# Output projection and ConvFFN as 2x2 blocks in seven products, with the gated activations in HBM between the FFN halves

## The chip, the core and the metric

The kernel runs on one core of one Trainium2 chip. The metric is the device time of one execution in microseconds (us). The engines are named as in the profile: PE (TensorE, matrix products; its weight loads are listed as PEld), DVE (VectorE), ACT (ScalarE), POOL (GpSimd) and SP (SyncE, whose queue issues every DMA of this kernel). PSUM is where PE writes its products, SBUF is the working memory of the core, HBM the memory outside.

## What is computed

One layer of a streaming encoder, for a prompt of 1024 tokens and 64 tokens of a running stream ("samples"), model width 1024. After two mixers (retention and gated linear attention, four heads each) come the parts that the change touches:

```
mix = concatenate([o_r, o_g])                         # 1024 wide
x   = x + g1 * (mix @ w_out)                          # w_out 1024 x 1024
h2  = rmsnorm(x) * (1 + sc2) + sh2
a, up = split(h2 @ w_ffn_in)                          # w_ffn_in 1024 x 5632, D_FF = 2816
conv = conv_b + sum_j conv_w[j] * a[t - 2 + j]        # causal, width 3
y   = silu(conv) * up
x   = x + g2 * (y @ w_ffn_out)                        # w_ffn_out 2816 x 1024
out = rmsnorm(x)
```

All inputs and outputs are fp32.

## The kernel before, in words

Activations are held with the features on the 128 partitions and the tokens as columns, in three chunks c of 384, 384 and 320 columns (the last one: 256 prompt tokens and the 64 samples). A product in nearly full precision takes three matmuls: operand and weight are each split into a high part (a rounded copy, by ACT) and a low part (the rest, a subtraction, by DVE or POOL), and `mm3` (line 247) issues high x high, high x low and low x high into one PSUM bank for each block of 128 features. All matmuls go through `mm` (line 238, the profile's L239), all transposes through `tr` (L244), and ACT, DVE and POOL instructions through one wrapper (L91), so the profile tells them apart by their tiles.

Weights come as units of 512 KB in their order of use (`plan`, lines 598 to 618): `load_unit` issues the DMA, `split_unit` the ACT copy, and its low part follows on DVE. A `flow` object counts estimated PE time as instructions are emitted and gives side streams (generators) a step whenever their delay has passed, so that norms, evictions and loads are emitted between products.

Around the change, in order of emission: the gate of retention head 3 is projected chunk by chunk, and `split_mix` (line 1365) splits the mixed features of each chunk that is ready. The output projection (lines 1454 to 1498) loops over chunks and, within a chunk, over the eight output blocks m; every block has its weight unit loaded again for each chunk (24 units). Its result is scaled by the gate G1 and added to x, which PE has transposed; squares are summed for the norm. When a chunk is complete, `norm2` (line 1418) starts as a side stream: the sum over partitions by PE, a reciprocal root in 12 small DVE instructions (`rsqrt_steps`), its broadcast by PE, and the split of the normed chunk. The next chunk's products run meanwhile.

The ConvFFN (lines 1644 to 1668) loops over 22 blocks f of 128 features, in pairs: `ev_a` and `conv` make the convolution branch, `ev_u` multiplies with the up projection and splits the result, and `ffn_out` (line 1554) multiplies the two blocks of the pair before with their rows of w_ffn_out and adds the scaled result into x2, which stays in SBUF. Only one pair of blocks of y exists at a time. In the last pair the squares and the final norm (`final`, line 1598) follow chunk by chunk.

## Time and profile before

| | |
|---|---|
| median of 3 runs | 1528.62 us (1527.5 to 1533.15) |
| span of the profiled execution, first to last instruction | 1527.1 us |
| PE busy | 1440.4 us, 94%, 9062 matmuls |
| DVE, ACT, POOL busy | 902.2, 486.7, 349.6 us |
| read from HBM, written | 98.23 MB, 5.29 MB |

The profile holds one execution; its own time is its span (the profile has no other time of it), and the median of the runs lies 1.5 us above that. Busy times of the engines overlap. A matmul's duration in the profile covers its passage through the array, and the next one starts before it ends, so the distance between starts tells how fast PE works. "Idle before, releaser" names what ended a wait.

### The profile page before, as it was taken

What the parts mean: (1) busy time and instruction counts of PE and PEld (TensorE: products, weight loads), DVE (VectorE), ACT (ScalarE), POOL (GpSimd) and SP (SyncE); (2) the same over time, 40 slices, a digit from 0 to 9 for tenths busy, and PEclk for the clock granted to TensorE, in tenths of its full rate; (3) what the DMA queues carried; (4) which work ended last, traced back from release to release, by engine and by line L of the source; (5) the groups of instructions that cost most, each with busy time, mean ns of one, the idle gap of its engine ahead of it and who ended that gap; (6) DMA issues with size and microseconds to landing.
All of it is one profiled execution on the core that took longest, in us unless ns stands there. A gap on an engine that the chain in (4) does not pass through costs nothing.

```text
span 1527.1 us, 22788 instructions
## 1 busy us (share of the span) xinstructions
PE 1440.4 (94%) x9062; PEld 1393.9 (91%) x9062; DVE 902.2 (59%) x1754; ACT 486.7 (32%) x979; POOL 349.6 (23%) x423
## 2 busy tenths in 40 slices
PE   5999888989989899899999999999999999999997
PEld 3778778879879899899999999999999999999996
DVE  6637878957885888567644445362535454444445
ACT  5635344433233325454412121212121212112136
POOL 3335424414332443222110000000010101010024
PEclk9999999999999999999999999999999999999999
DMA  8420102123223222454111110101111111111103
GB/s 257 156 62 15 56 9 67 42 82 99 87 87 99 79 81 67 148 149 135 54 42 42 42 56 29 55 29 56 56 39 46 42 42 56 41 43 42 42 2 118
DMA packets 128336, 104.98 MB, mean 69 GB/s; under 512 B 5129, under 2 KB 114535, under 8 KB 128231
## 3 DMA queue, kind: packets, MB, share of 16 engines
q1 hardware_dynamic: 128231, 103.53, 22.2%
q8 instruction: 71, 1.16, 0.3%
q14 instruction: 34, 0.28, 0.1%
HBM read 98.23 MB, written 5.29 MB: 68 GB/s over the span
## 4 chain that ended last, share of the span: by engine, by line
PE 70%; DVE 15%; issue 5%; ACT 3%; POOL 1%; DMA 0%; DVEq 0%; POOLq 0%; ACTq 0%
PE mm L239 38%; PE o L239 16%; PE sc L239 15%; DVE qbd L91 2%; DVE att L91 1%; DVE acc L91 1%; PE sc L244 1%; DVE t L91 1%; DVE ra L91 1%; DVE b L91 1%; DVE on L91 1%; ACT on L91 1%; DVE lo L91 1%; DVE sbd L91 1%; POOL acc L91 1%
## 5 line engine op out<-in xcount | busy, mean ns | idle before, releaser
L239 PE MATMUL mm<-act_hi,hi 128*128 128x384 f32 (+1 forms) x1152 | 393.0, 341 | 0.3 <-DVE mix L91 0.2
L239 PE MATMUL mm<-act_hi,lo 128*128 128x384 f32 (+1 forms) x1152 | 379.4, 329 | 4.2 <-DVE lo L91 4.2
L239 PE MATMUL mm<-act_lo,hi 128*128 128x384 f32 (+1 forms) x1152 | 378.7, 329 | 0.1
L239 PEld LDWEIGHTS mm<-act_hi,lo 128*128 128x128 f32 x1152 | 218.3, 190 | 4.7 <-DVE lo L91 4.5
L239 PEld LDWEIGHTS mm<-act_hi,hi 128*128 128x128 f32 x1152 | 219.3, 190 | 1.9 <-DVE mix L91 0.5
L239 PEld LDWEIGHTS mm<-act_lo,hi 128*128 128x128 f32 x1152 | 219.0, 190 | 0.8 <-POOL act_lo L91 0.3
L91 DVE TENSOR_TENSOR lo<-raw,hi 128x1024 fp32r<-128x1024 f32 x115 | 144.4, 1264 | 93.5 <-ACT hi L91 93.4
L91 ACT CAST hi<-raw 128x1024 fp32r<-128x1024 f32 x118 | 121.7, 1042 | 224.1 <-issue 192.4
L91 DVE TENSOR_SCALAR cv<-ab,cw 128x1090 f32<-128x1090 f32 x22 | 18.7, 849 | 188.0 <-ACT ab L91 186.3
L91 DVE SCALAR_TENSOR_TENSOR x<-mm,G,x 128x384 f32<-128x384 f32 (+2 forms) x201 | 95.7, 498 | 51.2 <-PE mm L239 39.5
L91 POOL TENSOR_TENSOR yl<-yf,yh 128x384 fp32r<-128x384 f32 (+1 forms) x66 | 63.1, 969 | 225.9 <-ACT yh L91 225.9
L91 POOL COPY tails<-ab 128x2 f32<-128x2 f32 x44 | 6.8, 189 | 459.4 <-ACT ab L91 459.4
L239 PE MATMUL sc<-act_hi,lo 128*128 128x384 f32 (+1 forms) x288 | 94.1, 327 | 0.0
L239 PE MATMUL sc<-act_lo,hi 128*128 128x384 f32 (+1 forms) x288 | 94.1, 327 | 0.0
L239 PE MATMUL sc<-act_hi,hi 128*128 128x384 f32 (+1 forms) x288 | 94.1, 327 | 0.0
L239 PE MATMUL o<-act_hi,lo 128*128 128x384 f32 (+1 forms) x288 | 93.7, 325 | 0.0
L239 PE MATMUL o<-act_hi,hi 128*128 128x384 f32 (+1 forms) x288 | 93.7, 325 | 0.0
L239 PE MATMUL o<-act_lo,hi 128*128 128x384 f32 (+1 forms) x288 | 93.6, 325 | 0.0
L239 PE MATMUL mm<-hi,act_hi 128*128 128x256 f32 x288 | 87.8, 305 | 0.2 <-ACT hi L91 0.2
L239 PE MATMUL mm<-lo,act_hi 128*128 128x256 f32 x288 | 82.6, 287 | 3.0 <-DVE lo L91 3.0
L239 PE MATMUL mm<-yh,hi 128*128 128x384 f32 (+1 forms) x254 | 84.1, 331 | 1.0 <-DVE na L91 0.6
L239 PE MATMUL mm<-yh,lo 128*128 128x384 f32 (+1 forms) x254 | 83.5, 329 | 0.0
(247 smaller groups left out, 3038.2 us busy)
## 6 DMA issues: line engine op xcount, KB each, us to landing
raw<-in_w_ffn_in_dram SPq DMA_DIRECT2D x44, 512.0 KB, 3.8
raw<-in_w_ada_dram SPq DMA_DIRECT2D x32, 512.0 KB, 4.0
raw<-in_w_in_dram SPq DMA_DIRECT2D x28, 512.0 KB, 3.8
raw<-in_w_out_dram SPq DMA_DIRECT2D x24, 512.0 KB, 3.9
raw<-in_w_ffn_out_dram SPq DMA_DIRECT2D x22, 512.0 KB, 4.7
wa<-in_w_ada_dram SPq DMA_DIRECT2D x16, 512.0 KB, 4.8
xs<-in_x_prompt_dram SPq DMA_DIRECT2D x8, 512.0 KB, 7.2
out_dram<-yt SPq DMA_DIRECT2D x8, 512.0 KB, 3.4
```

Of the source, the lines that this page charges most:

```text
L91: return call(*args, **kw)
L239: T.matmul(out, lhsT, rhs, start=start, stop=stop)
L244: T.transpose(out=out, in_=in_, identity=ident[0:n, 0:n])
```

## The change

The output projection, the FFN's in-projection and its out-projection each become a product of matrices in 2x2 blocks, done as seven products of half the size in each direction (Strassen's algorithm in Winograd's form), with sums and differences of the blocks of weights and activations as operands. The three chunks go away: tokens are held with the 64 samples in front and the 1024 prompt tokens behind (1088 columns).

- A class `OutProj` does both projections to the model width. Its steps are (product p, row block i) in the order 1, 2, 7, 6, 4, 5, 3; KH is 4 row blocks for the output projection and 11 for the FFN. A step multiplies a weight block of 128 x 512 with 512 tokens: four output blocks, three matmuls of 512 columns each. Combinations are made on POOL in place, `split` makes the high part on ACT and the low part on DVE, two steps ahead. The samples are multiplied beside it, with their tokens as the stationary operand (two matmuls of 512 columns in each step of products 1, 2, 4 and 5). Results of a product that enter several output blocks are added into x2 one by one on DVE. Norms are issued at fixed steps (`hooks`).
- The mixed features are copied into one tile B, which takes memory of the operands of the projections before. x comes in nine tiles of 128 tokens and is transposed before the first product.
- The FFN's in-projection takes all 1088 tokens in two halves of 544, in two PSUM banks of 272 columns. Seven operands X1 to X7 are made once from h2 (high and low parts). For each of 22 groups q (two feature blocks of the convolution branch, or of the up projection) there are seven products of 4 x 3 x 2 matmuls, in the order 1, 6, 5, 2, 7, 3, 4. The weight combinations are made on POOL and split four products ahead. `evict_in` adds the products up; the convolution follows for an even q, the gate for an odd one.
- The gated activations y go to HBM, a DMA for each feature block (`store_y`), and x2 too. After the in-projection y and x2 are loaded back, and then the FFN's out-projection runs over all 22 blocks at once.
- The weight units of these three products, `split_mix`, `norm2`, `ffn_out` and `final` of before go away; memory pools are closed and opened between the stages.

The new code, cut to its core:

```diff
+    proj(gate_ret(3))
+    act_ctx.close()
+    out_ctx = ExitStack()
+    bp = out_ctx.enter_context(tc.tile_pool(name="bp", bufs=1, side="right", reuse_waits="tile"))
+    B = bp.tile([P, KD, SEQ + SMP], F32, name="B")
...
+    ORD_OUT = (1, 2, 7, 6, 4, 5, 3)
+    class OutProj:
...
+        def prep(self):
+            p, i = self.steps[self.nprep]
+            self.nprep += 1
+            while self.nload < min(len(self.steps), self.nprep + self.nblk - 1):
+                self.load()
+            KH, b, cb = self.KH, self.b, self.cb[:, i]
+            blk = self.blk.pop((p, i))
+            if p == 1:
+                w = cb
+            elif p in (2, 4):
+                w = blk[0]
+            elif p == 7:
+                sub(cb, cb, blk[0])
+                w = cb
+            elif p == 6:
+                sub(cb, blk[0], cb)
+                w = cb
+            elif p == 5:
+                plus(blk[0], blk[0], cb)
+                w = blk[0]
+            else:
+                sub(blk[0], blk[0], cb)
+                w = blk[0]
+            b11, b12, b21, b22 = b(i, 0), b(i, 1), b(KH + i, 0), b(KH + i, 1)
+            if p == 1:
+                y = b11
+            elif p == 2:
+                y = b21
+                sub(b11, b12, b11)
+            elif p == 7:
+                sub(b12, b22, b12)
+                y = b12
+            elif p == 6:
+                y = self.ring.tile([P, 512], F32, tag="ys", name="ys", bufs=2)
+                sub(y, b22, b11)
+                sub(b21, b21, y, V)
+            elif p == 4:
+                y = b21
+            elif p == 5:
+                y = b11
+            else:
+                y = b22
...
+            split(cy, y)
+            split(cw, w)
...
+        def run(self):
+            KH = self.KH
+            ahead = min(self.ncw, self.ncy) - 1
+            sets, x1s, lazy = None, [], []
+            sb, ss = None, []
+            for n, (p, i) in enumerate(self.steps):
+                while self.nprep < min(len(self.steps), n + 1 + ahead):
+                    self.prep()
+                if i == 0 and p in (1, 7, 6, 5):
+                    sets = [pair(), pair()]
+                if i == 0 and p in (1, 4):
+                    sb = one()
+                if i == 0:
+                    ss += [next(self.samples) for _ in range({1: 2, 7: 1, 4: 1}.get(p, 0))]
+                    s = ss.pop(0) if p in (1, 2, 4, 5) else None
+                cw, cy = self.cw.pop((p, i)), self.cy.pop((p, i))
+                first = i == 0 and p in (1, 7, 6, 5)
+                last = i == KH - 1
+                for m in range(4):
+                    o = sets[m // 2][:, m % 2]
+                    ms = slice(m * P, (m + 1) * P)
+                    more = p in (2, 4, 3)
+                    mm(o, cw[:, 0, ms], cy[:, 0], first, False, more)
+                    mm(o, cw[:, 0, ms], cy[:, 1], False, False, more)
+                    mm(o, cw[:, 1, ms], cy[:, 0], False, last, more)
+                    if last:
+                        if p == 1:
+                            x1 = self.ring.tile([P, 512], F32, tag="x1", name="x1", bufs=4)
+                            S.copy(out=x1, in_=o)
+                            x1s.append(x1)
+                            lazy += [(m, 1, x1), (4 + m, 0, x1), (4 + m, 1, x1)]
+                        for mo, half in {1: (), 2: ((m, 0),), 7: ((4 + m, 1), (4 + m, 0)),
+                                         6: ((m, 1), (4 + m, 1)), 4: ((4 + m, 0),),
+                                         5: ((4 + m, 1),), 3: ((m, 1),)}[p]:
+                            self.evict(mo, half, o)
+                if p in (1, 2, 4, 5):
+                    a = p in (1, 4) and i == 0
+                    e = p in (2, 5) and last
+                    if a:
+                        mm(sb, s[:, i, :], cw[:, 0], True, False)
+                    mm(sb[0:SMP, :], s[:, i, 0:SMP], cw[:, 1], False, False)
+                    if not a:
+                        mm(sb, s[:, i, :], cw[:, 0], False, e)
+                    if e:
+                        self.sample(sb, 0 if p == 2 else 4)
+                if p == 2:
+                    for _ in range(-(-12 // KH)):
+                        if lazy:
+                            self.evict(*lazy.pop(0))
+                for fn in self.hooks.get((p, i), ()):
+                    fn()
...
+    def x_tile(t):
+        xt = abp.tile([P, D], F32, tag="cv" if t % 2 else "ab", name="xt", bufs=4)
+        n = P if t < 8 else SMP
+        nc.sync.dma_start(out=xt[0:n, :], in_=x_prompt[0, t * P:(t + 1) * P, :] if t < 8
+                          else x_sample[0])
+        pt = pair()
+        c0 = SMP + t * P if t < 8 else 0
...
+    def operand(p, half_k, half_t, pool):
+        t = X[p] = pool.tile([P, 2, 4, HT], F32R, name=f"X{p}", bufs=1)
+        for i in range(4):
+            src = hf[(4, 0)[half_k] + i][:, half_t * HT:half_t * HT + HT]
+            S.copy(out=t[:, 0, i], in_=src)
+            (V if i % 2 else G).tensor_tensor(out=t[:, 1, i], in0=src,
+                                              in1=t[:, 0, i].bitcast(F32), op=ALU.subtract)
...
+    hooks = {(5, 0): [partial(norm2, SMP, 512, 0)],
+             (3, 0): [partial(norm2, 0, SMP, 1), lambda: operand(1, 0, 0, xap),
+                      lambda: operand(2, 1, 0, xap)],
+             (3, 3): [partial(norm2, SMP + 512, 512, 0), store_x2]}
...
+    for t in range(9):
+        x_tile(t)
+    hf = [abp.tile([P, 2 + T2], F32, tag="ab" if k < 4 else "cv", name="h2f", bufs=4)
+          for k in range(KD)]
+    op1.run()
...
+    for i in range(4):
+        sub(h2(i, 0), h2(i, 1), h2(i, 0), V if i % 2 else G)
+    operand(5, 0, 0, xbp)
+    for i in range(4):
+        sub(h2(i, 1), h2(4 + i, 1), h2(i, 1), V if i % 2 else G)
+    operand(7, 0, 1, xbp)
+    operand(3, 1, 1, xbp)
+    for i in range(4):
+        sub(h2(4 + i, 1), h2(4 + i, 1), h2(i, 0), V if i % 2 else G)
+    operand(6, 1, 1, xbp)
+    for i in range(4):
+        sub(h2(4 + i, 0), h2(4 + i, 1), h2(4 + i, 0), V if i % 2 else G)
+    operand(4, 1, 0, xbp)
...
+    ORD_IN = (1, 6, 5, 2, 7, 3, 4)
...
+        if p == 6:
+            s1 = sums[q, 1] = new()
+            plus(s1, a21, a22)
+            s2 = sums[q, 2] = new()
+            sub(s2, s1, a11)
+            w = s2
+        elif p == 7:
+            w = new()
+            sub(w, a11, a21)
+        elif p == 3:
+            w = new()
+            sub(w, a12, sums[q, 2])
+        else:
+            w = {1: a11, 2: a12, 4: a22}.get(p)
+            if w is None:
+                w = sums[q, 1]
+        t = combos[q, p] = fw.tile([P, 2, 4, P], F32R, tag="wc", name="wc", bufs=4)
+        split(t, w)
...
+    def evict_in(q, p):
+        f = q // 2 * 2
+        if p == 1:
+            chain["a"] = chain["o"]
+            S.copy(out=view(dst(q, 0, 0)), in_=chain["a"][:, :, 0:HQ])
+        elif p == 6:
+            V.tensor_tensor(out=view(dst(q, 0, 1)), in0=chain["o"][:, :, 0:HQ],
+                            in1=view(dst(q, 0, 0)), op=ALU.add)
+        elif p == 5:
+            S.copy(out=view(dst(q, 1, 1)), in_=chain["o"][:, :, 0:HQ])
+        elif p == 7:
+            V.tensor_tensor(out=view(dst(q, 1, 0)), in0=chain["o"][:, :, 0:HQ],
+                            in1=view(dst(q, 0, 0)), op=ALU.add)
+            S.copy(out=view(dst(q, 0, 0)), in_=chain["a"][:, :, 0:HQ])
+            plus(dst(q, 1, 1), dst(q, 1, 1), dst(q, 1, 0))
+        elif p == 3:
+            V.tensor_tensor(out=view(dst(q, 0, 1)), in0=chain["o"][:, :, 0:HQ],
+                            in1=view(dst(q, 0, 1)), op=ALU.add)
+            if q % 2 == 0:
+                conv(f, 0)
             else:
+                gate_y(f, 0)
+        elif p == 4:
+            V.tensor_tensor(out=view(dst(q, 1, 0)), in0=view(dst(q, 1, 0)),
+                            in1=chain["o"][:, :, 0:HQ], op=ALU.subtract)
+            if q % 2 == 0:
+                conv(f + 1, 1)
+            else:
+                gate_y(f + 1, 1)
+        if q % 2 and p == 1:
+            silu(f, 0)
+        if q % 2 and p == 5:
+            silu(f + 1, 1)
+        if q % 2 == 0 and q and p == 6:
+            store_y(f - 2, 0)
+        if q % 2 == 0 and q and p == 5:
+            store_y(f - 1, 1)
...
+    n_prep = 0
+    ps_of = {}
+    for s, (q, p) in enumerate(steps):
+        while n_prep < min(len(steps), s + 4):
+            prep_in(*steps[n_prep])
+            n_prep += 1
+        if q % 2 == 0 and p == ORD_IN[0]:
+            for n in range(2):
+                abt[q // 2, n] = abp.tile([P, 2 + T2], F32, tag="ab", name="ab", bufs=4)
+        grp = {1: "A", 2: "A", 6: "B", 7: "B", 5: "C", 3: "C", 4: "D"}[p]
+        first = p in (1, 6, 5, 4)
+        if first:
+            ps_of[grp] = pair()
+        o = chain["o"] = ps_of[grp]
+        t, x = combos.pop((q, p)), X[p]
+        for k in range(4):
+            for a, b in ((0, 0), (0, 1), (1, 0)):
+                for c in range(2):
+                    mm(o[:, c, 0:HQ], t[:, a, k, :], x[:, b, k, c * HQ:(c + 1) * HQ],
+                       first and k == 0 and a + b == 0, k == 3 and a == 1, not first)
+        evict_in(q, p)
...
+    hooks = {(5, 2): [partial(final, SMP, 512, 0)],
+             (3, 2): [partial(final, 0, SMP, 8)],
+             (3, KF - 1): [partial(final, SMP + 512, 512, 4)]}
+    for f in range(KF):
+        load_y(f, 0)
+        if f == 2:
+            load_ys(0, KF)
+            load_ys(KF, KF)
+    for f in range(KF):
+        load_y(KF + f, 0)
+    nc.sync.dma_start(out=x3, in_=d_x2)
+    for f in range(KF):
+        load_y(f, 1)
+    for f in range(KF):
+        load_y(KF + f, 1)
+    op2 = OutProj(fo, KF, lambda k, h: Y[:, k, h * 512:h * 512 + 512],
+                  lambda k: w_ffn_out[0, k * P:(k + 1) * P, :], x3, G2,
+                  sample_parts(fo, ysm[:, 0:KF], ysm[:, KF:NF], KF), hooks, 3, 3, 3)
+    op2.run()
```

Here B[:, 0:4] holds the four heads of the gated linear attention and B[:, 4:8] those of the retention, `pair()` is one of three pairs of PSUM banks and `one()` one of two single banks. `sub` and `plus` run on POOL unless an engine is given. `load_y` and `load_ys` are DMAs of 256 KB and 32 KB issued by SP, `stats` (called by the norms) sums eight squares, on DVE and POOL in turn, and `load` issues DMAs of 256 KB for the weight blocks, nblk - 1 = 2 steps ahead of `prep`.

## Rows read from the trace of the kernel before

**Rows 1.** The page: busy time by engine, busy tenths in 40 slices.

```profile
PE 1440.4 (94%) x9062; PEld 1393.9 (91%) x9062; DVE 902.2 (59%) x1754; ACT 486.7 (32%) x979; POOL 349.6 (23%) x423
...
PE   5999888989989899899999999999999999999997
...
DVE  6637878957885888567644445362535454444445
...
POOL 3335424414332443222110000000010101010024
```

**Rows 2.** Windows: us, busy PE, PEld, DVE, ACT, POOL, clock, DMA share, GB/s.

```profile
603.00:700.00 97.00, 92.10 (x558) 90.56 (x557) 63.32 (x101) 48.66 (x86) 28.58 (x29) 0.96 0.50 151
617.00:621.00 4.00, 4.00 (x13) 4.00 (x13) 1.92 (x3) 2.36 (x5) 0.00 (x0) 0.50 0.45 134
700.00:1512.00 812.00, 810.64 (x4936) 809.21 (x4935) 387.05 (x665) 191.53 (x322) 97.84 (x180) 1.00 0.15 46
1512.00:1527.10 15.10, 5.67 (x41) 4.24 (x39) 7.28 (x24) 6.65 (x13) 3.22 (x4) 0.85 0.51 191
```

**Rows 3.** Timeline, PE: start us, us; first and last of unbroken runs of one width.

```profile
115.11 0.28 PE L239 MATMUL mm<-hi,act_hi 128*128 128x256 f32 x1
...
117.15 0.28 PE L239 MATMUL mm<-hi,act_lo 128*128 128x256 f32 x1
...
592.86 0.33 PE L239 MATMUL mm<-act_hi,hi 128*128 128x384 f32 x1
...
599.10 0.31 PE L239 MATMUL mm<-act_hi,hi 128*128 128x320 f32 x1
...
600.41 0.49 PE L244 MATMUL sc<-ident,on 128*128 128x128 f32 x3
```

**Rows 4.** Groups by form, 720 to 1512 us: busy us, mean ns of one.

```profile
L91 ACT CAST hi<-raw 128x1024 fp32r<-128x1024 f32 x64 | 65.7, 1043 | 213.8 <-issue 192.4 <-PE mm L239 21.4
L91 DVE TENSOR_TENSOR lo<-raw,hi 128x1024 fp32r<-128x1024 f32 x65 | 78.5, 1221 | 63.9 <-ACT hi L91 63.9
L91 DVE SCALAR_TENSOR_TENSOR cv<-ab,cw,cv 128x1090 f32<-128x1090 f32 x44 | 59.6, 1355 | 1.6
L91 DVE SCALAR_TENSOR_TENSOR x<-mm,G,x 128x384 f32<-128x384 f32 x85 | 52.3, 617 | 31.1 <-PE mm L239 31.1
L91 DVE SCALAR_TENSOR_TENSOR x<-mm,G,x 128x256 f32<-128x256 f32 x40 | 19.3, 483 | 8.4 <-PE mm L239 8.4
L91 POOL TENSOR_TENSOR yl<-yf,yh 128x384 fp32r<-128x384 f32 x44 | 43.7, 1013 | 174.0 <-ACT yh L91 174.0
```

**Rows 5.** Groups by form, 602 to 614 us: low parts on DVE and POOL together.

```profile
L91 DVE TENSOR_TENSOR act_lo<-mix,act_hi 128x384 fp32r<-128x384 f32 x7 | 9.1, 1350 | 0.0
L91 POOL TENSOR_TENSOR act_lo<-mix,act_hi 128x384 fp32r<-128x384 f32 x7 | 9.0, 1325 | 0.0
```

**Rows 6.** Timeline, DVE: first and last of the 12 instructions of a reciprocal root.

```profile
688.80 0.15 DVE L91 TENSOR_SCALAR vv<-st 128x3 f32<-128x3 f32 x1
...
690.97 0.16 DVE L91 SCALAR_TENSOR_TENSOR nr<-na,nr 128x3 f32<-128x3 f32 x1
```

**Rows 7.** Timeline, PE: the wait at 612 us and the matmuls behind it.

```profile
616.69 0.69 PE L239 MATMUL mm<-act_hi,lo 128*128 128x384 f32 x1 [4.23 <-DVE lo L91]
617.17 0.53 PE L239 MATMUL mm<-act_hi,hi 128*128 128x384 f32 x1
```

**Rows 8.** Windows with dense DMA (columns as in rows 2), and the page's GB/s by slice.

```profile
4.00:20.00 16.00, 5.44 (x21) 2.45 (x21) 8.31 (x14) 9.72 (x13) 4.62 (x2) 1.00 1.03 332
...
40.00:46.00 6.00, 6.00 (x43) 5.05 (x42) 2.48 (x3) 5.48 (x8) 1.52 (x2) 1.00 1.06 372
...
GB/s 257 156 62 15 56 9 67 42 82 99 87 87 99 79 81 67 148 149 135 54 42 42 42 56 29 55 29 56 56 39 46 42 42 56 41 43 42 42 2 118
```

**Rows 9.** The page's DMA issues: KB each, median us from issue to landing.

```profile
raw<-in_w_in_dram SPq DMA_DIRECT2D x28, 512.0 KB, 3.8
...
xs<-in_x_prompt_dram SPq DMA_DIRECT2D x8, 512.0 KB, 7.2
```

More of the change, by code (lines that the diff above doesn't have):

```diff
@@ new lines, in stream_step_kernel @@
+    for i in range(4, 8):
+        for c in range(NC3):
+            o, n = B[:, i, c * CW:c * CW + WID[c]], mix[c][KORD[i]][:, 0:WID[c]]
+            if (i + c) % 2:
+                V.tensor_copy(out=o, in_=n)
+            else:
+                S.copy(out=o, in_=n)
+    attn_ctx.close()
+    early_ctx.close()
+    psum_ctx.close()
+    T2 = SEQ + SMP
+    HT = T2 // 2
+    HQ = HT // 2
+    ps2 = ctx.enter_context(tc.tile_pool(name="ps2", bufs=3, space=PSUM, reuse_waits="tile"))
+    ps1 = ctx.enter_context(tc.tile_pool(name="ps1", bufs=2, space=PSUM, reuse_waits="tile"))
@@ new lines, in stream_step_kernel, with split, sub, plus @@
+    V.tensor_tensor(out=fold64, in0=ident[:, 0:SMP], in1=ident[:, SMP:P], op=ALU.add)
+    def split(dst, src, eng=None):
+        S.copy(out=dst[:, 0], in_=src)
+        (eng or V).tensor_tensor(out=dst[:, 1], in0=src, in1=dst[:, 0].bitcast(F32),
+                                 op=ALU.subtract)
+    def sub(out, a, b, eng=None):
+        (eng or G).tensor_tensor(out=out, in0=a, in1=b, op=ALU.subtract)
+    def plus(out, a, b, eng=None):
+        (eng or G).tensor_tensor(out=out, in0=a, in1=b, op=ALU.add)
@@ new lines, in sample_parts @@
+    def sample_parts(pool, a, b, kh):
+        for n in range(4):
+            if n == 2:
+                sub(b, b, a)
+            src = b if n in (1, 2) else a
+            t = pool.tile([P, kh, 2 * SMP], F32R, tag="sp", name="sp", bufs=2)
+            S.copy(out=t[:, :, 0:SMP], in_=src)
+            V.tensor_tensor(out=t[:, :, SMP:2 * SMP], in0=src, in1=t[:, :, 0:SMP].bitcast(F32),
+                            op=ALU.subtract)
+            yield t
+    ffn0 = ExitStack()
+    xap = ffn0.enter_context(tc.tile_pool(name="xap", bufs=1, reuse_waits="tile"))
@@ new lines, in norm2 @@
+    def norm2(a, n, j):
+        rstd, w, nt = stats(x2, a, n, "n")
+        pb = one()
+        for i in range(nt):
+            mm(pb[:, i * P:i * P + w], rstd[:, i:i + 1].broadcast_to([w, P]), ident[0:w, 0:w],
+               True, True)
+        for k in (4, 5, 6, 7, 0, 1, 2, 3):
+            o = hf[k][:, a:a + n]
+            V.scalar_tensor_tensor(out=o, in0=x2[:, k, a:a + n], scalar=A2[:, k, j:j + 1],
+                                   in1=pb[:, 0:n], op0=ALU.mult, op1=ALU.mult)
+            S.activation(out=o, in_=o, func=AF.Identity, bias=B2[:, k, j:j + 1])
```

547 lines of the change are left out of this document (241 added, 306 removed).

## The prediction

> **What bounds the kernel now.** I read the page first, for the share of each engine [rows 1]: TensorE (PE) is busy 94% of the span, and from the 21st of 40 slices on its digit is 9 in every slice, while DVE stands at 2 to 6 and POOL mostly at 0 or 1. Then the busy time by stage [rows 2]: the output projection with the second norm lies between 603 and 700 us, the ConvFFN between 700 and 1512, the last norm behind it. In the ConvFFN PE is busy 810.6 of 812 us at the full clock, so its time is a count of matmuls times their distance, and nothing that other engines do there costs anything. Third, the distance [rows 3]: 36 matmuls of 384 columns start within 6.24 us (173 ns each), 9 of 320 within 1.31 us (146 ns), 17 of 256 within 2.04 us (120 ns). Distance is thus about columns / 2.4 GHz plus 13 ns. Hence I take 126 ns for 272 columns (a little above 256) and 228 ns for 512 (173 and 128 columns more at 0.43 ns).
>
> **What the products save.** Before, 592 pairs of weight block and feature block (64 output, 352 in, 176 out) each take three products of 384, 384 and 320 columns: 592 x 3 x (0.1733 x 2 + 0.1456) = 874 us. After: output projection 7 x 4 x 4 x 3 = 336 matmuls of 512, and 32 for the samples, which both projections to the model width multiply block by block: 368 x 0.228 = 83.9 us. FFN in: 22 x 7 x 4 x 3 x 2 = 3696 of 272 columns x 0.1264 = 467.2 us. FFN out: 924 + 88 = 1012 of 512 x 0.228 = 230.7 us. Together 781.8 us, 92 less. The columns fall by 11.4% (1.932 to 1.712 million), so the change does what it says on PE. It is paid for where PE has no work: the old code interleaves each norm, split and load with products of another chunk; the new one has seams at which a whole half or the whole activation must be ready.
>
> **Prices at the seams** [rows 4]: ACT copy of 512 columns 0.62 us (half of 1.043 at 1024 and a fixed part), DVE subtraction of 512 0.64 (half of 1.221 and a fixed part), DVE eviction of 512 0.75 (0.617 at 384, 0.483 at 256), DVE on 1088 from SBUF 1.36, POOL add or subtract of 512 1.35 (1.013 at 384, in proportion). Where DVE and POOL subtract at the same time they take turns: both need 1.34 us for 384 columns [rows 5] where each alone needs 0.5 to 1.0; I take 1.88 for a pair of 544. A reciprocal root is 12 small instructions in 2.3 us [rows 6]. After a gap of 4.2 us PE runs at the 1.2 GHz level for about 4 us (13 matmuls in it) [rows 2, 7]; I charge 2 us for each new long gap. DMA moved 332 GB/s from 4 to 20 us, where loads stand in a queue, 372 in the densest six us and 257 over the first slice [rows 8].
>
> **The sum, from 603 us**, when head 3's gate ends (all before it is unchanged):
>
> *Seam A, +20.* The copies into B wait until the projections' operands are freed, since B takes their memory; the x tiles land where the mixes lay: about 3 us until the loads start. Nine x loads (4.46 MB) stand on SP's queue before the first output weights: 13.4 us. Then the weights' landing (a free 512 KB load takes 3.8 us, partly hidden) and a split, 3.6. The 72 transposes run inside this wait. Bounds 14 and 26.
>
> *Output projection, +83.9, and its stalls, +34.* Evictions come in eights after products 7 and 6, 6 us of DVE against a step of 2.74, and product 4 accumulates into banks that must be read first: 5. Two sample folds wait for an ACT copy: 2. The norm of half 0 (issued in product 5's first step): eight squares and seven adds on DVE and POOL in turn (4 x 0.64 + 3 x 1.35, with handoffs 7.5, after two copies and a first square) end 9.9 us after product 4; PE has 3.2 us of work, then waits 6.7, then 2.3 for the root, and 2 for the sums, broadcast and late splits: 11. The samples' norm: 5.5. The operands X1 and X2 (four pairs at 1.88 on DVE and POOL) stand on DVE's queue before the next split: 5.5. Clock: 5. Bounds 18 and 50.
>
> *Seam B, +49.* After product 3 the second half's squares, adds, root, broadcast and eight scalings (8 x 0.75) end at 16.4 us. Product 6 of the first FFN block needs X6, before which DVE and POOL must do 12 combinations and 16 low parts, 14 pairs x 1.88 = 26.3; X4's 8 more (7.5) and the two weight sums of product 6 (2.7, POOL) stand in the same queues ahead of its split (1.3). POOL starts some 2 us early: 52 us, of which product 1 covers 3. The store of x2 (4.46 MB, about 13 us) is done by then. Nearest bounds: 38 (no taking turns, 14 + 4 pairs at POOL's 1.44, and an earlier norm) and 60.
>
> *FFN in, +467.2 and 2 of clock.* Per two blocks (42.5 us of PE) DVE has 14 splits, 8 evictions, two convolutions of 3.9 and a gate: about 24 us; ACT 14, POOL 19. The evictions are hidden by the three pairs of banks and the splits are three products (9 us) ahead. If this cover fails, see the rivals. The stores (22 of 557 KB) and the 88 weight loads share a queue at about 60 GB/s; a store waits for its gate there, with the next weights behind it, which are some 20 us early.
>
> *Seam C, +55.* The last gate and store are issued 2.2 us after the last product. Only then does SP issue the reload, Y (44 x 256 KB), the samples (0.72 MB) and x2 (4.46 MB), 16.7 MB, because nothing of it is issued earlier and Y takes the memory of the FFN operands; the first output weights stand behind all of it. 16.7 MB at 332 GB/s is 50.3, their landing and split 2.5. That a load waits for those before it is seen where equal 512 KB loads need 7.2 us in a burst and 3.8 us alone [rows 9]. Bounds: 49 at 372 GB/s and 70 at 257; 8 if the weights did not wait. The Trainium skill, in DMA: Bandwidth & Descriptors, section Specifications, gives 435 GB/s as the ceiling of the fabric; by it (an estimate) this term would be 43 and the total 12 us lower, but the densest stretch is below it, and I keep 332.
>
> *FFN out, +230.7, and its stalls, +37.* The final norm of half 0 is issued in product 5: squares, adds and then eight more scalings on ACT hold PE for 7 us, and four tiles pass through the one free pair of banks, 17 together. Samples' norm 8, evictions 5, folds 2, clock 5. Bounds 22 and 50.
>
> *End, +20* behind the last product, where 15 us are spent now [rows 2]: the last piece is four tiles rather than three, and its sum of squares starts later.
>
> 603 + 20 + 83.9 + 34 + 49 + 469.2 + 55 + 230.7 + 37 + 20 = 1601.8 us of span, against 1527.1 now. The median of the runs, 1528.62, is 1.5 above that span, hence **1603 us**, 4.9% slower: 92 us are gained, and about 195 us of seams and stalls replace about 30 us of transposes, gaps and tail.
>
> **Rivals.** *DVE or POOL binds FFN in.* On blocks with convolutions DVE holds 15 us of 21 and POOL's four combinations may take turns with it; if product 2's split comes 1 to 3 us late in each of the 11 pairs of blocks, that is 10 to 35 us: about 1630. For it: the taking turns [rows 5]. Against: POOL's combinations are ready blocks ahead and most DVE operations read PSUM. Chance 0.17.
>
> *The seams are shorter than their sums.* If engines run ahead in their queues so that A, B, C and the stalls reach the low ends (14, 38, 49, 18, 22), the sum is 1548: still slower. Chance 0.14.
>
> *Not slower: wide products come closer together than their columns.* Place: the 1380 matmuls of 512 columns. If they came every 175 ns instead of 228, as the 384 ones do now, 73 us go away and the total is 1530; below 165 it is faster. Against it, the distance grows steadily from 256 to 320 to 384 columns [rows 3]. Chance 0.05. Beside it: the Trainium skill, TensorE: Matmul & The Clock Gate, section Back-to-back issue gap, states 131 ns for a stream of 512-column matmuls with their weight loads; by that (an estimate) the total would be 1469. The trace does not agree: 173 ns at only 384 columns.
>
> My forecast, seams and stalls about as summed, has 0.60 (1575 to 1630); 0.04 is for a seam that I have misread altogether and that vanishes.
>
> **Numbers.** Slower by over 0.5% (about what a measurement here can tell): 0.60 + 0.17 + 0.14 = 0.91; faster 0.05 and same 0.04, from the last two cases. The range 1548 to 1648 reaches from the short seams to the worst DVE case.
>
> **What would show it.** Matmuls 9062 to about 8800; distances of 126 and 228 ns; PE idle for some 20 us at 603, 45 to 50 before FFN in and 50 to 55 before FFN out, the last ended by the DMA of w_ffn_out, with DMA near full there; the gap before FFN in ended by DVE or POOL; idle spells of some 10 us in product 5 of both projections. Wrong: PE gaps in FFN in's steady state, weights that land soon after the last store, or a 512-column distance far below 228.

## The result, and the profile after

The changed kernel takes 1765.74 us (median of 4 runs, 1761.63 to 1766.57) where the kernel before takes 1529.92 beside it: a ratio of 1.1533, 95% interval 1.1512 to 1.1553. It is slower, as forecast, but by 15.3% and not by 4.9%: the time lies 118 us above the range. The profiled execution has a span of 1759.6 us.

The page of the changed kernel, where [rows 1] shows the kernel before; the last line is the granted clock of TensorE in tenths:

```profile
PE 1423.6 (81%) x8842; PEld 1284.8 (73%) x8842; DVE 1118.2 (64%) x1858; ACT 599.4 (34%) x1178; POOL 650.8 (37%) x549
...
PE   5998888999998867651899999999999149888686
...
DVE  6648788677678676568655556665566125786454
...
POOL 3434334343243052227343443443343021951232
PEclk9999999999999987775899999999999669899798
```

PE's digit was 9 in every slice of the second half but the last; now there are two holes (slice 19, slices 32 and 33), with slices of 5 to 8 ahead of the first and, mostly, behind the second. GpSimd (POOL), which was idle in most of that half, stands mostly at 2 to 4, and the clock is lower wherever PE has holes. The same in windows, one for each term of the forecast's sum (columns as in [rows 2]: seam A, output projection, seam B, FFN in, seam C, FFN out, end):

```profile
602.00:619.60 17.60, 10.44 (x73) 8.98 (x73) 8.65 (x18) 11.13 (x25) 0.00 (x0) 0.90 0.88 309
619.60:788.50 168.90, 116.05 (x404) 86.04 (x404) 110.00 (x167) 54.93 (x107) 54.89 (x39) 0.79 0.10 35
788.50:836.00 47.50, 4.91 (x19) 3.92 (x18) 37.98 (x44) 20.83 (x34) 32.64 (x21) 0.50 0.42 139
836.00:1371.00 535.00, 490.00 (x3698) 485.06 (x3698) 317.72 (x385) 154.09 (x242) 213.09 (x189) 0.95 0.19 61
1371.00:1430.70 59.70, 0.15 (x2) 0.00 (x0) 3.10 (x5) 1.23 (x3) 1.26 (x1) 0.53 0.87 317
1430.70:1738.10 307.40, 263.45 (x1078) 204.41 (x1078) 193.08 (x256) 111.08 (x203) 124.37 (x83) 0.92 0.21 71
1738.10:1759.60 21.50, 8.57 (x42) 7.63 (x40) 8.39 (x21) 10.80 (x17) 3.79 (x3) 0.62 0.27 98
```

Set against the sum, term by term (the first counted from 603 us):

| term | forecast | measured | difference |
|---|---|---|---|
| seam A | 20 | 16.6 | -3.4 |
| output projection | 83.9 + 34 | 168.9 | +51.0 |
| seam B | 49 | 47.5 | -1.5 |
| FFN in | 467.2 + 2 | 535.0 | +65.8 |
| seam C | 55 | 59.7 | +4.7 |
| FFN out | 230.7 + 37 | 307.4 | +39.7 |
| end | 20 | 21.5 | +1.5 |

The three seams and the end are right to within 5 us each. All but 1.3 us of the miss, 156.5 us, lies inside the three stages of products. It is idle time and slow time in about equal parts: the projection has 168.9 - 116.1 = 53 us of idle PE (34 were forecast for all stalls) and 116 us of busy PE for what was forecast at 84, at a mean clock of 0.79; in all three stages 69 us more idle and 88 more busy. Of the busy time 8 us in the projection and 14 in FFN out are small matmuls (folds of the samples, norms, transposes), which the sum has in part among its stalls.

The distances are as forecast. In FFN out twelve matmuls of 512 columns start within 2.73 us, 227.5 ns each (timeline of PE; the last line only ends the stretch):

```profile
1605.55 2.89 PE L240 MATMUL d<-cy,cw 128*128 128x512 f32 x12
1608.28 0.62 PE L240 MATMUL s<-cw,sp 128*64 128x512 f32 x2
```

So the products do cost what the sum says, and the rival of wide products closer together falls. The Trainium skill, TensorE: Matmul & The Clock Gate, section Back-to-back issue gap, has 131 ns for such a stream; these rows disagree with it.

What holds PE, from the list of its waits (us in total, times, longest):

```profile
PE d L240 <- ACT cw L91: 67.5, 3, 59.6
PE d L240 <- DVE x L91: 51.1, 24, 11.0
PE d L240 <- DVE wc L91: 37.0, 12, 3.3
...
PE d L240 <- ACT wc L91: 32.0, 1, 32.0
...
PE d L240 <- DVE ab L91: 7.9, 11, 0.7
```

The first and the fourth are, for 59.6 and 32.0 us, seams C and B. Of the other three the sum had 10 us for evictions and nothing else: 24 waits for evictions into x, 12 for a weight split in FFN in, 11 for an eviction into ab.

**FFN in.** The gaps recur every 47.8 us, 11 times, where a pair of blocks was forecast at 42.5. One of them in the timeline:

```profile
1010.51 2.74 DVE L91 SCALAR_TENSOR_TENSOR cv<-ab,cw,cv 128x1088 f32<-128x1088 f32 x2
...
1015.38 3.75 PE L240 MATMUL d<-X,wc 128*128 128x272 f32 x28 [0.72 <-DVE ab L91]
1015.43 1.88 POOL L91 TENSOR_TENSOR ws<-wr 128x512 f32<-128x512 f32 x1
1016.21 4.55 DVE L91 SCALAR_TENSOR_TENSOR cv<-ab,cw,cv 128x1088 f32<-128x1088 f32 x2
1017.28 2.33 POOL L91 TENSOR_TENSOR ws<-wr,ws 128x512 f32<-128x512 f32 x1
...
1021.42 0.68 DVE L91 TENSOR_TENSOR wc<-wr,wc 128x512 fp32r<-128x512 f32 x1
...
1022.16 2.08 PE L240 MATMUL d<-X,wc 128*128 128x272 f32 x11 [3.04 <-DVE wc L91]
```

Two taps of the first convolution take 2.74 us, the same two of the second take 4.55, because POOL forms sums of weights beside them. Behind them on VectorE's queue stands the split at 1021.42, and PE waits for it. The 28 matmuls before the wait are product 5's 24 and four of product 2: those that need only the high part. So it is product 2's split that is late.

**The ends of products.** Product 7 of the output projection:

```profile
683.98 1.65 POOL L91 TENSOR_TENSOR ys<-B 128x512 f32<-128x512 f32 x1 [0.63 <-DVE cy L91]
684.43 1.40 DVE L91 SCALAR_TENSOR_TENSOR x<-d,G,x 128x512 f32<-128x512 f32 x2
685.88 2.93 PE L240 MATMUL d<-cy,cw 128*128 128x512 f32 x6 [3.98 <-DVE x L91]
687.57 2.73 DVE L91 SCALAR_TENSOR_TENSOR x<-d,G,x 128x512 f32<-128x512 f32 x4 [1.74 <-PE d L240]
690.35 2.08 PE L240 MATMUL d<-cy,cw 128*128 128x512 f32 x4 [1.54 <-DVE x L91]
```

PE doesn't wait for an operand here. After output block m = 0 it stops until VectorE has read that block twice, does m = 1 and 2 (six matmuls), and stops again. Blocks 0 and 1 are the two halves of one two-bank PSUM tile, as are 2 and 3. VectorE comes to block 0 only at 684.43, when it is done with product 6's operands.

**The clock.** Two neighbouring stretches of the projection, and the stretch around seam B:

```profile
654.50:675.00 20.50, 11.26 (x29) 8.18 (x30) 13.74 (x21) 1.92 (x4) 5.91 (x5) 0.50 0.09 30
675.00:685.20 10.20, 6.91 (x31) 5.38 (x29) 9.32 (x13) 3.42 (x6) 5.92 (x4) 1.00 0.15 48
777.40:836.00 58.60, 10.80 (x30) 7.36 (x30) 44.29 (x50) 23.33 (x38) 35.46 (x23) 0.50 0.34 113
```

Behind the 11 us wait at the end of product 2, 29 matmuls (eight of them of 64 columns) hold PE for 11.26 us at the 1.2 GHz level; 31 take 6.91 at the full one. The clock row of the page stands at 7 and 8 in the slices of the projection (15 to 18), where a wait stands at the end of every product.

### The profile page after: what moved, and what is told of

Same layout as the page of the kernel before. It is cut to its first block, busy times and chain, and to the rows that moved or that the text cites. A ratio compares the mean times of both kernels' runs of the same rounds, so it can differ in the third digit from the quotient of the medians.

```text
span 1759.6 us, 23428 instructions
## 1 busy us (share of the span) xinstructions
PE 1423.6 (81%) x8842; PEld 1284.8 (73%) x8842; DVE 1118.2 (64%) x1858; ACT 599.4 (34%) x1178; POOL 650.8 (37%) x549
## 5 line engine op out<-in xcount | busy, mean ns | idle before, releaser
L240 PE MATMUL d<-X,wc 128*128 128x272 f32 x3696 | 489.9, 296 | 77.0 <-DVE wc L91 37.0
L240 PEld LDWEIGHTS d<-X,wc 128*128 128x128 f32 x3696 | 484.9, 196 | 81.9 <-DVE wc L91 39.8
L240 PE MATMUL d<-cy,cw 128*128 128x512 f32 x1260 | 339.7, 422 | 125.5 <-ACT cw L91 67.5
L240 PEld LDWEIGHTS d<-cy,cw 128*128 128x128 f32 x1260 | 252.5, 204 | 200.1 <-ACT cw L91 68.4
L240 PE MATMUL mm<-act_hi,hi 128*128 128x384 f32 (+1 forms) x480 | 170.5, 355 | 0.3 <-DVE mix L91 0.2
L240 PE MATMUL mm<-act_lo,hi 128*128 128x384 f32 (+1 forms) x480 | 158.5, 330 | 0.1
L240 PE MATMUL mm<-act_hi,lo 128*128 128x384 f32 (+1 forms) x480 | 158.5, 330 | 0.0
L240 PEld LDWEIGHTS mm<-act_hi,hi 128*128 128x128 f32 x480 | 92.2, 192 | 1.9 <-DVE mix L91 0.5
L240 PEld LDWEIGHTS mm<-act_lo,hi 128*128 128x128 f32 x480 | 91.9, 191 | 0.7 <-POOL act_lo L91 0.3
L240 PEld LDWEIGHTS mm<-act_hi,lo 128*128 128x128 f32 x480 | 91.4, 190 | 0.0
```

The source lines that it names most:

```text
L240: T.matmul(out, lhsT, rhs, start=start, stop=stop, skip_group_check=more)
```

## Experiments

The first four change one thing each. All runs but the last are single ones, beside the kernel before at 1528.8 to 1532.3 us; they are compared by stages, whose lengths repeat to 1 to 3 us where nothing was changed (the start of the projection varies more, from 615.6 to 622.4 us). A stage runs from its first to its last wide matmul.

### Blocks in tiles of one bank

```diff
                 if i == 0 and p in (1, 7, 6, 5):
-                    sets = [pair(), pair()]
+                    sets = [bank6() for _ in range(4)]
...
-                    o = sets[m // 2][:, m % 2]
+                    o = sets[m]
```

> Edit: in the output projection and in FFN out the four output blocks of a product lie in four PSUM tiles of one bank each (six banks in turn) in place of two tiles of two banks. The changed kernel takes 1765.7 us. Theory A (at a product's last step the second block of a two-bank tile waits until VectorE has read the first, because the tile is one unit for the waits): the waits of 4.37 + 2.17 us at the end of product 7, 3.07 + 2.17 of product 6, 1.94 + 1.23 of product 4 and 3.07 + 1.24 of product 5 go, about 45 us in both halves together, and with them part of the half clock; output projection 168.8 to 140-145 us, FFN out 307.4 to 275-285, the run about 1705-1715. Rival B (VectorE is behind at these places anyway): the same wait comes one or two steps later, before a split, and the run stays above 1750.

The transposes go to single banks too. Measured: 1705.6 us, 60 less. Output projection 137.9, FFN out 281.6, FFN in unchanged (534.4). The list of waits has

```profile
PE d L240 <- DVE x L91: 12.3, 11, 4.7
```

where it had 51.1 us in 24 waits; 5 us came back as waits for splits. Theory A: VectorE has the same work, and PE no longer stops for most of it, so the tile was the unit of waiting. One place is different, the end of the projection's product 2 (11.05 us before). There VectorE is behind with the late additions of product 1's copies (`x<-x`), and 4.69 of the 12.3 us stay. The same trace shows that evictions, one of whose two inputs is in PSUM, don't slow down beside GpSimd:

```profile
656.47 4.10 DVE L91 SCALAR_TENSOR_TENSOR x<-x,G,x 128x512 f32<-128x512 f32 x3
...
661.69 2.71 DVE L91 SCALAR_TENSOR_TENSOR x<-d,G,x 128x512 f32<-128x512 f32 x4
661.90 1.27 POOL L91 TENSOR_TENSOR cb<-wb,cb 128x512 f32<-128x512 f32 x1 [1.88 <-issue]
...
662.49 2.07 PE L240 MATMUL d<-cy,cw 128*128 128x512 f32 x4 [4.69 <-DVE x L91]
```

Four evictions in 2.71 us, 0.68 each, with POOL at its own 1.27. Operations with both inputs in SBUF take 1.7 to 1.8 us on both engines when they meet (product 6 below).

### The convolution handed out

```diff
-        V.scalar_tensor_tensor(out=cv[:, 0:T2], in0=ab[:, 1:T2 + 1], scalar=cwv(1, f),
-                               in1=cv[:, 0:T2], op0=ALU.mult, op1=ALU.add)
...
+        late.extend([tap0, partial(tap, 1), rest])
...
+        for _ in range({(0, 3): 2, (0, 4): 2, (1, 1): 1, (1, 6): 1}.get((q % 2, p), 0)):
+            late.pop(0)()
```

> Edit: in FFN in the three taps of each convolution are handed out over the products after it (two after product 3, two after product 4, one each after products 1 and 6 of the next block) in place of six operations at once. Theory A (the burst of two convolutions delays the splits that stand behind them on VectorE): the gaps of 1.0 and 3.3 us in each of the 11 pairs of blocks go, and the half clock after them; the period of a pair falls from 47.8 us to 42.5-43.5, FFN in from 534.6 to 470-482, the run to 1708-1720. Rival B (VectorE and GpSimd together have too much work, wherever it stands in the period): the gaps move to another product, the period stays above 46 and the run above 1745.

Measured: 1699.6 us, 66 less; FFN in 471.3. PE has no gap left in the steady part: 430 of 430 us in the window, 3409 matmuls, 126.1 ns each (126.4 in the forecast).

```profile
870.00:1300.00 430.00, 430.00 (x3409) 427.88 (x3408) 287.95 (x358) 138.42 (x224) 193.53 (x172) 1.00 0.23 73
```

Theory A, with a time below its 1708 to 1720. VectorE and GpSimd have the same work as before, and it fits.

### The sums of weights left out

```diff
-        if p == 6:
-            s1 = sums[q, 1] = new()
-            plus(s1, a21, a22)
...
+        w = {1: a11, 2: a12, 6: a21, 7: a11, 3: a12, 5: a21, 4: a22}[p]
```

> Edit: in FFN in the three sums and differences of weights of a block on GpSimd are left out, the blocks' raw weights are split in their place (so the values of FFN in are others); the convolution stays in one burst. In the changed kernel two operations of the second convolution take 2.26 and 2.25 us beside GpSimd's 1.88 and 2.33 us operations, in place of 1.35. Theory A (the burst itself stalls, the taking turns adds 1.8 of the 4.3 us): the gap stays at about 2 us a pair, the period falls from 47.8 to 45-46.5, the run to 1735-1750. Rival B (the taking turns is the whole stall): no gap, period 42.5-43, the run 1708-1715.

Measured: 1694.3 us, FFN in 467.5, no gap in the steady part, with the convolutions still in one burst. That is rival B, with a time below its 1708 to 1715: the burst alone doesn't stall. The mean tap, in groups by form of FFN in, first of the changed kernel, then of this one:

```profile
L91 DVE SCALAR_TENSOR_TENSOR cv<-ab,cw,cv 128x1088 f32<-128x1088 f32 x44 | 75.8, 1722 | 1.6
```

```profile
L91 DVE SCALAR_TENSOR_TENSOR cv<-ab,cw,cv 128x1088 f32<-128x1088 f32 x44 | 59.5, 1352 | 1.6
```

Together with the run before: the stall needs both the burst and the turns with GpSimd inside it. Either one taken away removes all of it.

### Loads by need

```diff
     for f in range(KF):
+        op2.load()
         load_y(f, 0)
-        if f == 2:
+        if f == 0:
             load_ys(0, KF)
             load_ys(KF, KF)
     for f in range(KF):
+        if f < 3:
+            op2.load()
         load_y(KF + f, 0)
+        load_y(f, 1)
```

> Edit: ahead of FFN out the loads stand in the order of use (weight block and activation block of product 1 side by side, then product 2's, the residual behind them) in place of all activations and the residual ahead of the first weight block. Theory A (the 59.9 us ahead of FFN out are one queue's 16.7 MB ahead of the first weights): the stretch falls to 8-15 us and nothing of it comes back, since product 1 then needs 0.5 MB in each 2.7 us; the run 1715-1725. Rival B (the bytes bind, at the measured 332 to 375 GB/s): products 1 and 2 wait for blocks, half of the gain or more is given back, the run 1740-1755.

Measured: 1726.4 us, 39 less. The 59.7 us ahead of FFN out become 9.2, but FFN out grows from 307.4 to 320.4. PE in the timeline:

```profile
1382.44 5.35 PE L240 MATMUL d<-cy,cw 128*128 128x512 f32 x12 [8.68 <-ACT cw L91]
1398.99 1.22 PE L240 MATMUL s<-cw,sp 128*128 128x512 f32 x2 [11.20 <-DVE sp L91]
```

Theory A by the mechanism, though 13 us come back and its 1715 to 1725 is missed by 1; neither theory named the 11.2 us: 22 small loads of sample columns now stand between, and the samples' split waits for the last. Products 1 and 2 were not starved, with up to 405 GB/s moved beside them (1420 to 1440 us).

### The three together, and the projection's late additions

The first run joins the single banks, the convolution handed out and the loads by need. The second also spreads the late additions of product 1's copies:

```diff
-                if p == 2:
-                    for _ in range(-(-12 // KH)):
+                if p in (2, 7, 6):
+                    for _ in range(1 if KH == 4 else 2):
```

> Edit: the single-bank blocks (e1_banks), the spread convolution (e2_spread) and the loads by need (e3_reload) together. One at a time they took 60, 66 and 39 us off 1765.7. Theory A (three separate stalls in three stages): the gains add up, 1595-1606 us, with 136-140 us for the output projection, 467-472 for FFN in, 9-10 ahead of FFN out and 282-296 for FFN out. Rival B (they share a resource, VectorE and GpSimd, and each gain frees time that another stall then takes): 1620 or more.

> Edit: c1_three, and in the output projection the 12 late additions of product 1's copies come one a step over products 2, 7 and 6 in place of three a step in product 2. Theory A (three a step put VectorE behind by the end of product 2, which leaves waits of 1.59 and 5.09 us there): these waits go, 8-12 us with the half clock after them, 130 us or less for the output projection. Rival B (VectorE's work in the projection is the limit): the waits come at products 7 and 6, and the stage stays within 4 us of c1_three's.

Measured: 1604.0 us for the three. 1765.7 - 60 - 66 - 39 is 1600.7: the stalls add up (theory A), with 137.1, 472.3, 9.5 and 298.4 us for the four stages named. With the late additions spread 1608.0, projection 138.4 us: rival B. The distances of 1.60 and 5.08 us between matmuls at the end of product 2 went, and others of 0.99, 1.68, 3.78 and 2.03 us came in products 7 and 6.

### VectorE alone

```diff
-            (V if i % 2 else G).tensor_tensor(out=t[:, 1, i], in0=src,
+            V.tensor_tensor(out=t[:, 1, i], in0=src, in1=t[:, 0, i].bitcast(F32),
...
-            plus(sqs[:, 0:n], sqs[:, 0:n], sq[:, 0:n], V if k % 2 else G)
+            plus(sqs[:, 0:n], sqs[:, 0:n], sq[:, 0:n], V)
...
-    steps = [(q, p) for q in range(NQ) for p in ORD_IN]
+    ORD_0 = (1, 5, 6, 2, 7, 3, 4)
+    steps = [(q, p) for q in range(NQ) for p in (ORD_IN if q else ORD_0)]
```

> Edit: c2_lazy, and around the norms: the sums of squares and all operands of FFN in on VectorE alone in place of VectorE and GpSimd by turns; weight blocks of products 1, 5 and 6 split ahead of the operands, these three products of the first block ahead of the operands of 7, 3 and 4. In the changed kernel an operation on 544 columns takes 1.8 us beside GpSimd's and 0.7 alone. Theory A (by turns the two engines get no more done than VectorE alone): product 1 starts 10-18 us earlier and the first block ends 10-18 us earlier, each norm's statistics 2-3 us shorter, the run 18-30 us below c2_lazy. Rival B (GpSimd's share is real work taken off VectorE): VectorE is the longer of the two now, and the run is within 5 us of c2_lazy or above it.

In the second run also every difference inside the two projections: `sub(cb, blk[0], cb)` becomes `sub(cb, blk[0], cb, V)`, and so on.

> Edit: c3_seams, and in both OutProj halves every sum and difference of blocks on VectorE, none on GpSimd. In FFN out a step of product 6 takes 4.0 us with two differences on GpSimd and one on VectorE beside two splits. Theory A (the pair of engines works by turns, so VectorE alone needs 5 x 0.7 us): product 6's step 3.5 us, the run 3-10 us below c3_seams. Rival B (GpSimd does add capacity where VectorE has only splits to do): products 7, 2, 5 and 3 get slower steps, the run 5-20 us above c3_seams.

Measured: 1588.0 and 1578.3 us, 20 and 10 less, both in theory A's ranges. In the first, FFN in starts 27 us sooner after the projection, of which 18 are given back in its first block, which now waits for operands 7, 3 and 4 (net 9); the output projection is 9 us shorter. Part of that is the new order and not the engine, which this run doesn't separate. The second run changes the engine alone: FFN out gets 5.9 us shorter (294.5 to 288.6), the projection gains nothing (129.4 and 130.5), so theory A holds for FFN out only; the rest of the 10 us lies ahead of the projection and in small differences elsewhere. One step of product 6 in FFN out with GpSimd, then on VectorE alone:

```profile
1419.23 1.67 POOL L91 TENSOR_TENSOR ys<-Y 128x512 f32<-128x512 f32 x1 [0.63 <-DVE cy L91]
1419.68 1.77 DVE L91 TENSOR_TENSOR Y<-Y,ys 128x512 f32<-128x512 f32 x1
1420.87 1.74 POOL L91 TENSOR_TENSOR cb<-wb,cb 128x512 f32<-128x512 f32 x1
1421.38 1.78 DVE L91 TENSOR_TENSOR cy<-ys,cy 128x512 fp32r<-128x512 f32 x1
1423.08 0.68 DVE L91 TENSOR_TENSOR cw<-cb,cw 128x512 fp32r<-128x512 f32 x1
1423.23 1.67 POOL L91 TENSOR_TENSOR ys<-Y 128x512 f32<-128x512 f32 x1 [0.62 <-DVE cy L91]
```

```profile
1404.80 0.69 DVE L91 TENSOR_TENSOR Y<-Y,ys 128x512 f32<-128x512 f32 x1
...
1408.06 0.69 DVE L91 TENSOR_TENSOR Y<-Y,ys 128x512 f32<-128x512 f32 x1
```

A step is 4.0 us with both engines (1419.23 to 1423.23) and 3.26 with one. Five operations of 0.65 on VectorE are done sooner than three there beside two on GpSimd.

### More cover, and fewer products by sevens

Three more runs look for a version that beats both kernels. The first puts work into the waits at the seams:

```diff
-    for t in range(9):
-        x_tile(t)
+    for t in range(9):
+        hooks.setdefault((1, t // 2) if t < 8 else (2, 0), []).append(partial(x_tile, t))
...
+    in_parts(hooks, norm2(SMP, 512, 0), (5, 0), (5, 2), (5, 3))
+    in_parts(hooks, norm2(0, SMP, 1), (5, 3), (3, 0), (3, 0))
```

The second and third make the output projection, then FFN out too, by eight products, each block summed over all k in one bank: `op1 = PlainProj(` for `op1 = OutProj(`, and `op2` likewise.

> Edit: c4_alone, and the waits at the seams given work: the residual's nine transposes stand between the steps of the output projection's product 1 (not ahead of it), each norm comes in three parts at three steps of products 5 and 3 (sums of squares, root, scaling), the activations' sample columns go to HBM tensors of their own and come back in two loads in place of 22. Theory A (TensorE waits at these places only for what could have been issued earlier): the 17 us ahead of product 1 fall to 4-8, the waits of 6.15 + 2.87 + 4.33 + 2.52 us at the norms in the output projection and 4.58 + 1.96 in FFN out to under 6 in all, the 11.3 us at the samples of FFN out to 2-4; 1538-1552 us after 1578.3. Rival B (VectorE's queue is full there, and the parts wait as long in their new places): 1565 or more.

> Edit: d0_cover with the output projection by eight products (each output block's sum over all eight k in one PSUM bank, one eviction, no sums of blocks) in place of seven. Eight take 384 + 32 matmuls of 227.5 ns, 94.6 us, seven take 336 + 32, 83.7. Theory A (in the projection, where a product has only 4 steps, the sums, copies and evictions of Strassen cost TensorE more in waits than the eighth product): the stage from the first to the last 512-column matmul 100-110 us, the run 8-20 us below d0_cover. Rival B (the waits were those of the norms and the covers, which d0_cover has dealt with): the run 8-12 us above d0_cover.

> Edit: d1_plainout with FFN out by eight products too, so that only FFN in is by seven. Eight take 1056 + 88 matmuls, 260.3 us, seven 924 + 88, 230.2. Theory A (with 11 steps in a product the sums are mostly covered; the waits left over are 25-35 us, product 6's slow steps and the evictions): FFN out 262-270 us, the run within 8 us of d1_plainout on either side. Rival B (the covers of d0_cover leave nothing to gain here): the run 20-30 us above d1_plainout.

Measured: 1564.6, 1554.2 and 1589.9 us. In the first the wait ahead of the projection is 9.6 us and the samples' in FFN out 2.3, but the samples' norm in the projection still holds PE for 6.2 + 4.0 us, since its parts follow each other closely (argued from the order of the parts, not tested). The time misses theory A's range by 13 us and stands at the bound of rival B. In the second the eighth product is cheaper than the waits it replaces (theory A's 8 to 20: 10.4 less; the stage falls from 135.0 to 123.2 us), though 123.2 is above the 100 to 110 expected; the transposes are inside it. The third has a wait of its own making: all but three weight blocks stand behind the whole reload,

```profile
1299.57 2.93 PE L240 MATMUL d<-cy,cw 128*128 128x512 f32 x6 [30.51 <-ACT cw L91]
```

so 35.7 us more than the second is no answer. Without those 30.5 it would be 5 above, with some 282 us for FFN out where theory A had 262 to 270; that wasn't run. The best version, 1554.2 us with only the FFN by seven products, is 1.4% above the kernel before (1532.3 in the same series). None beat it.

### The two stalls alone

> Edit: the single-bank blocks (e1_banks) and the spread convolution (e2_spread) together, nothing else; the loads ahead of FFN out stay as the change has them. This is the change with the two stalls taken out that the prediction did not have. Theory A (these two are most of the miss; gains of 60 and 66 us add up): 1635-1645 us, which lies in the range of the prediction (1548 to 1648) with some 37 us over its 1603, 18-20 of them in the output projection (half clock and the end of product 2) and 12-15 in FFN out. Rival B (c1_three's sum came out only because the loads by need were there too): 1655 or more.

Measured: 1642.9 us (median of 4, 1640.9 to 1645.5), ratio to the kernel before 1.0724, interval 1.0693 to 1.0755. Theory A: with these two taken out the change lies in the forecast's range, near its top. Output projection, FFN in, FFN out:

```profile
617.90:755.00 137.10, 106.56 (x404) 80.74 (x404) 107.43 (x167) 54.27 (x106) 58.58 (x39) 0.86 0.13 43
803.00:1275.50 472.50, 469.59 (x3698) 466.96 (x3697) 308.95 (x386) 148.77 (x241) 210.82 (x188) 0.99 0.22 69
1335.00:1617.80 282.80, 254.93 (x1078) 198.91 (x1078) 200.25 (x256) 110.03 (x201) 129.71 (x83) 0.96 0.23 77
```

FFN in is then 3 us over its forecast (469.2), the projection 19 (117.9) and FFN out 15 (267.7). The idle time of these two, 30.5 and 27.9 us, is no longer above the stalls forecast (34 and 37). What is left over is busy time, 23 us above the products' price in the projection and 24 in FFN out: 7 and 13 of that are the small matmuls, and some 16 and 12 are products at a clock of 0.86 and 0.96.

## Why the prediction was wrong, and where it was right

**Right: the products and the seams.** 92 us fewer of products, 227.5 ns and 126.1 ns, about 8800 matmuls (8842), and every seam to 5 us. Seam B is made of the turns on VectorE and GpSimd that [rows 5] had shown (1.8 us for a pair of 544 columns), and seam C of the order of one queue, as in [rows 9]; its wait is put down to ACT's copy, which stands behind the first weight block's load, and the run with loads by need confirms the order as the cause.

That both came out to 5 us is in part luck:

```profile
836.06 1.27 PE L240 MATMUL d<-X,wc 128*128 128x272 f32 x4 [32.01 <-ACT wc L91]
L1872 SPq DMA_DIRECT2D ysm<-d_y x22: 429/430/439, 1377.3 to 1387.2; - x22
1400.00:1430.00 30.00, 0.00 (x0) 0.00 (x0) 0.00 (x0) 0.00 (x0) 1.26 (x1) 0.50 1.03 403
```

In seam B the wait stands ahead of product 1, which was to cover 3 us of it: its weight split comes behind all seven operands on ACT's queue. The norm's scalings end 19.9 us after product 3 and not 16.4, but product 6's weight sums, priced inside the seam, come behind 836. In seam C the reload is issued 4.9 us after the last product (2.2 forecast), and SP then needs 10.4 us to issue the 22 small loads of sample columns, which the sum had by their bytes only (68 GB/s moved from 1381 to 1386). The rest came faster than priced: 403 GB/s from 1400 to 1430, above the 332. The Trainium skill, DMA: Bandwidth & Descriptors, section Specifications, gives 435 GB/s as the ceiling of the fabric; by it (an estimate) the term was 43 us. It measured 59.7, and the rate in its dense part is nearer to that ceiling than to 332.

**Wrong, 65.8 us: "The evictions are hidden by the three pairs of banks and the splits are three products (9 us) ahead."** This was a sum over two blocks: 24 us of VectorE in 42.5. Measured it is 28.9, and 24.5 where GpSimd's sums are left out: the turns were not in it. The work does fit on average, as the run with the convolution handed out shows. But it was written as a burst, with both convolutions and two POOL sums in the same 12 us, and VectorE's rows come in the order written. The prediction had the place: its first rival said product 2's split, 11 times, by turns. It gave that 0.17 and 10 to 35 us because "POOL's combinations are ready blocks ahead"; the timeline has them right beside the second convolution. The size failed too: 3.3 us late is just above the "1 to 3" it allowed, but there is 1.0 us more at product 5 (ab), and the price left out the half clock behind each gap: 5.3 us a pair, 58 in all; the rest is mainly the start of the first block, with a wait of 2.8 us and half the clock behind seam B.

**Wrong, some 60 us: evictions after products, "5" in each projection.** The sum counted VectorE's work at the end of a product and not what an eviction locks. Block 1 waits for block 0's eviction because both are in one tile: 39 us of waits (51.1 to 12.3) and 60 us of time went with the single banks, where the two projections had 10 for it. Part of this is the 11.05 us at the end of product 2, where VectorE is also behind with the late additions, which the sum had nowhere; spread over more steps they made PE wait elsewhere.

**Wrong: "I charge 2 us for each new long gap".** In [rows 2, 7] one isolated gap was followed by 4 us at half the clock. Behind the 11 us wait in the projection, with shorter waits after it, the low level lasts from 662 to 675. The sum had 5, 2 and 5 us of clock in the three stages; without the small matmuls, the products held PE some 24, 24 and 19 us longer than at their full distance. In the run without the two stalls it is 16, 3 and 12, which makes half of the 37 us that this run's span is over the forecast; the small matmuls, priced only in part, are much of the rest. No run changes the clock alone.

**Also not foreseen:** product 6's step in FFN out, 4.0 us for 2.73, where five operations on two engines take turns.

The chances: "slower" at 0.91 was right, from the seams. The top of the range, 1648, was to be the worst case of one rival, whose 35 us give 1638; all rivals were about other places than the ends of products, so nothing in the range stood for them.

## What to carry to other kernels

A cover that holds on average has to be checked in the order of the queue: write down what one engine executes between two deadlines, and with whom it takes turns there. Look at each PSUM tile for who waits on the whole of it; blocks that are evicted one by one belong in tiles of one bank. An algorithm that saves an eighth of the products pays with sums, evictions and seams, and a wait it leaves can cost more than its length: in the two projections 39 us of idle time went with the single banks and 17 of busy time with it, and in FFN in 4.3 us of delay cost 5.3. Here the 92 us saved were not enough in any version. Count the DMAs on a queue and not only their bytes: 22 small loads held the one queue for 10.4 us.

## What the runs showed of the hardware

GpSimd's help to VectorE was worth less than nothing in product 6 of FFN out, where both read two SBUF operands: 3.26 us alone, 4.0 together. Where VectorE's second operand is in PSUM neither slows down (0.68 and 1.27 us). The Trainium skill, SBUF — State Buffer, section Who interferes with whom, says both: a VectorE instruction with two SBUF inputs contends with a GpSimd instruction that reads SBUF, one with at most one SBUF input (outside the 2-port performance modes) does not. These rows agree; the prediction had seen the turns in [rows 5] but used them as a price at the seams, and not as a reason to take the work off GpSimd.
